# Gates and branch projections computed token-major, and a depthwise convolution issued tap by tap, in a three-layer hybrid block

## The chip, the cores and the metric

One core of a Trainium2 chip runs the whole program as one launch. The metric is the device time of one execution in microseconds (us); lower is better. TensorE (PE) does the matrix products, VectorE (DVE), ScalarE (ACT) and GpSimd (POOL) the rest; SP issues nearly all DMAs.

## The reference, cut to what matters

A sequence of 256 tokens of width 1024 goes through two layers of one kind (attention, gated linear attention and memory attention, then an MLP) and one layer of another (called layer 2 here: a spatial gate, a convolution and an attention). All three layers end their mixing part in the same way: three branches of width 512 are projected to 1024 columns, each is multiplied by a gate, the three are summed, and the sum is projected once more. In the first two layers the gate has a bias:

```python
gates = sigmoid(merge.reshape(B, S, 3, D) + b_merge)      # merge: 3072 of the columns of h @ w_in
merged = (gates[:, :, 0] * (o_nsa @ w_branch[0]) + gates[:, :, 1] * (o_gla @ w_branch[1])
          + gates[:, :, 2] * (o_mem @ w_branch[2]))
x = x + merged @ w_out
```

In layer 2 the gate is `sigmoid(h @ w_in[...])` without a bias, and branch 1 comes from a causal depthwise convolution over tokens, 31 taps on 512 channels, with a layer norm over the channels behind it.

## The kernel before, in words

**Precision and units.** Every product is done in three matmuls: both operands are split into a high part and a rest, `hi` and `lo`, and high times high, high times rest and rest times high are summed in PSUM (`mm3`, line 194). A weight arrives in a *unit*: 128 partitions of 1024 floats, 512 KB, one DMA from SP into `raw` (4 buffers). `split` (line 429) makes `hi` from it, on ACT or for every sixth unit on POOL (line 433), and `lo` by a subtraction on DVE (line 439), into 4 buffers each. While the convolution is being issued (`conv_on`), `hi` is never made on POOL, and every fourth subtraction goes to POOL (line 437).

**Two ways to multiply.** `tok_major` (line 489) holds 128 tokens of the activation in the array and streams weight columns past, up to 512 at a time, into two PSUM tiles (`acc`, 4 buffers), one for each half of the 256 tokens. `transposed` (line 503) holds 128 weight columns in the array and streams the 256 tokens past. A unit is consumed by 12 matmuls of 512 columns in the first way and by 24 of 256 in the second. The result of the second way has channels on the partitions, as the next product needs it; the result of the first has tokens there.

**Gates and branches.** `gates_of` (line 1123, layers 0 and 1) computes a gate of 1024 columns in four calls of `transposed`, 8 units in all; DVE scales the result by each token's norm (`RB`), and ACT takes the tanh with the bias (`CBH`, columns of `COL`, loaded as rows at the start). Layer 2 does the same at line 1587 without scale and bias. `merge_branch` (line 1135) projects a branch of 512 in four calls of `transposed`, 4 units in all. For each call DVE multiplies by the gate (line 1145 or 1147) and POOL adds into `M` (line 1148); on the last branch ACT and DVE split `M` into `mg`, which the output projection `out_proj` (line 1153, token-major) holds in the array, k after k. There are three gates and three branches in each of three layers.

**Order of the work.** PE's instructions run in the order written. The attentions and other side chains are generators; a planner (`clock`, `pump`, `start`, `finish`, `need`) counts an assumed time for each matmul and puts the next piece of a chain into PE's order when its assumed latency is over. The other engines' orders are made by a list scheduler at build time from priorities in program order, assumed durations and readiness, and are fixed from then on.

**The convolution.** `conv` (line 1427) is such a chain in layer 2. Its 120 taps run on DVE, all 30 of one channel block before those of the next, two for each step of the planner (1500 ns). Behind them stand the layer norm and the activation; the result is wanted before the last branch of layer 2 (`finish(c_conv)`, line 1592).

Of the kernel before, what the change touches and what calls it, by code (L numbers as in the profile page):

```python
# [10 lines left out]
F32 = mybir.dt.float32  # L11
# [87 lines left out]
def block_kernel(ctx, tc, x_in, mem_in, positions, ln_mix, w_in, b_merge, nsa_q_norm, nsa_k_norm,  # L99
# [173 lines left out]
    def load_rows():  # L273
# [3 lines left out]
        rows(48, 48, b_merge.rearrange("l b (k p) -> (l b k) p", p=P))  # L277
# [53 lines left out]
    CBH = consts.tile([P, 48], F32, name="CBH")  # L331
# [4 lines left out]
    def late_cols():  # L336
        pt = PS()
        tr(pt[:, :128], ROWB, IDF)
        dve.tensor_copy(COL[:, 48:128], pt[:, 48:128])
        dve.memset(COL[0:16, 102:110], 1.0)  # L340
        dve.memset(COL[64:80, 102:110], 1.0)
        dve.tensor_scalar(CBH, COL[:, 48:96], 0.5, None, op0=OP.mult)
# [84 lines left out]
    conv_on = [False]  # L427

    def split(hi, lo, raw):
        u = ucount[0]  # L430
        ucount[0] += 1
        if u % 6 == 5 and not conv_on[0]:
            pool.tensor_scalar(hi, raw, 1.0, 1.0, op0=OP.mult, op1=OP.mult)  # L433
        else:
            act(hi, raw, AF.Copy)  # L435
        if conv_on[0] and u % 4 == 0:
            pool.tensor_tensor(lo, raw, f32(hi), op=OP.subtract)  # L437
        else:
            dve.tensor_tensor(lo, raw, f32(hi), op=OP.subtract)  # L439
# [23 lines left out]
    def units(w2d, r0, nk, cols, paired=None, fine=False):  # L463
        n = sum(c1 - c0 for c0, c1 in cols)
        if paired:
            c0, c1 = cols[0]
            srcs = [(slice(64 * j, 64 * j + 64), 0, n,
                     w2d[256 * j:256 * j + 256, c0:c1].rearrange("(a d) n -> d a n", d=64)) for j in range(2)]
            h, lo = unit(srcs, 4, n)
            return [(h[:, j, :], lo[:, j, :]) for j in range(4)]  # L470
        per = max(1, 1024 // n)
# [17 lines left out]
    def tok_major(hh, hl, w2d, r0, nk, cols, fine=False):  # L489
        n = sum(c1 - c0 for c0, c1 in cols)  # L490
        ps = [ACC(), ACC()]
        ws = units(w2d, r0, nk, cols, None, fine)
# [630 lines left out]
    def gates_of(l, b, hh, hl, RB):  # L1123
        g = B8("gate")
        for c in range(4):
            ps = transposed(hh, hl, w_in[l], 0, 8, 3368 + 1024 * b + 256 * c, ACC())
            tmp = T2("gtmp", (2, 256))
            dve.tensor_tensor(tmp, v2(ps), RB[:, None, :].to_broadcast([P, 2, 256]), op=OP.mult)
            for j in range(2):
                cb = 2 * c + j  # L1130
                bc = l * 24 + b * 8 + cb
                act(g[:, cb, :], tmp[:, j, :], AF.Tanh, scale=0.5, bias=CBH[:, bc:bc + 1])
        return g

    def merge_branch(w2d, oT, g, M, last, mg, rows=None):
        oh, ol = oT
        first = M is None
        if first:
            M = B8("M")
        for c in range(4):  # L1140
            ps = transposed(oh, ol, w2d, 0, 4, 256 * c, ACC(), rows)
            cs = slice(2 * c, 2 * c + 2)
            fl = lambda t: t[:, cs, :].rearrange("p a b -> p (a b)")
            if first:
                dve.scalar_tensor_tensor(fl(M), fl(g), 1.0, ps, op0=OP.add, op1=OP.mult)
            else:
                dve.scalar_tensor_tensor(fl(g), fl(g), 1.0, ps, op0=OP.add, op1=OP.mult)  # L1147
                pool.tensor_tensor(fl(M), fl(M), fl(g), op=OP.add)  # L1148
                if last:
                    hilo(fl(mg[0]), fl(mg[1]), fl(M), 0.5)  # L1150
# [37 lines left out]
    def layer(l, hT):  # L1188
# [85 lines left out]
        for b in (2, 1, 0):  # L1274
            g = gates_of(l, b, hh, hl, RB)
# [101 lines left out]
    def layer_2(hT):  # L1377
# [49 lines left out]
        def conv():  # L1427
            conv_on[0] = True
            for cb in range(4):
                dve.tensor_scalar(CV[:, cb], GLU[:, cb, 0:256], CWT[:, cb, 0:1], COL[:, 110 + cb:111 + cb],  # L1430
                                  op0=OP.mult, op1=OP.add)
                for t in range(1, 31):
                    dve.scalar_tensor_tensor(CV[:, cb], GLU[:, cb, t:t + 256], CWT[:, cb, t:t + 1], CV[:, cb],
                                             op0=OP.mult, op1=OP.add)
                    if t % 2 == 0:
                        yield 1500.0
            conv_on[0] = False
            yield 1500.0
# [147 lines left out]
        for bi, b in enumerate((2, 0, 1)):  # L1586
            g = B8("gate")
            for c in range(4):
                ps = transposed(hh, hl, w, 0, 8, 5120 + 1024 * b + 256 * c, ACC())
                act(g[:, 2 * c:2 * c + 2, :], v2(ps), AF.Tanh, scale=0.5)  # L1590
# [92 lines left out]
```

## Time and profile before

| what | value |
|---|---|
| time, median of 3 runs (lowest to highest) | 1246.87 us (1245.86 to 1249.62) |
| the profiled execution's own time | 1243.95 us |
| its span, first to last instruction | 1242.2 us |
| PE busy, share of the span | 98% |
| weight loads of PE, DVE, ACT, POOL busy | 88%, 68%, 48%, 19% |
| matmuls | 8317 |
| mean granted TensorE clock | 0.995 of full |
| moved by DMA | 211 MB, 170 GB/s |

The busy time of PE counts modelled ends of pipelined matmuls, so two matmuls in a row overlap in it. What a matmul costs in a stream is the distance from its start to the next one's.

### The profile page before, as it was taken

To read this page: it belongs to the slowest core of one execution; us is meant where nothing else is said; L and a number is where in the kernel's file an instruction comes from. 1 tells how busy PE (TensorE), PEld (TensorE's weight loads), DVE (VectorE), ACT (ScalarE), POOL (GpSimd) and SP (SyncE) were. 2 spreads that over 40 slices of the span, in tenths; PEclk is the share of its full clock that TensorE was granted. 3 is DMA by queue.
4 is the path that set the end of the run, shared out by engine and by line. 5 is a ranking of instruction groups with operands and counts; after the bars stand their busy time and mean duration, and the time that the engine had idled before them with its cause. 6 is when DMAs were issued, how large, how long until landed. Compare 5 with 4: busy or idle time off the path is not lost. (4 is left out here: it accounts for less than half of the span.)

```text
span 1242.2 us, 21154 instructions
## 1 busy us (share of the span) xinstructions
PE 1216.0 (98%) x8317; PEld 1096.3 (88%) x8317; DVE 847.6 (68%) x1368; ACT 597.7 (48%) x957; POOL 239.8 (19%) x245
## 2 busy tenths in 40 slices
PE   8999999999999999999999999999999998999997
PEld 5897789998899898888689998989998987899996
DVE  5867888666745555667878557654545899955856
ACT  7567544444644344556654434534434334443542
POOL 2300220212112112200220023212211122110213
PEclk9999999999999999999999999999999999999999
DMA  8557523566566666656624565566665654455672
GB/s 277 173 159 204 157 91 109 171 183 214 167 187 184 193 185 189 184 157 171 188 69 115 154 187 185 173 200 180 193 190 170 199 154 131 134 173 169 186 218 72
DMA packets 165559, 211.00 MB, mean 170 GB/s; under 512 B 12065, under 2 KB 132277, under 8 KB 165460
## 3 DMA queue, kind: packets, MB, share of 16 engines
q1 hardware_dynamic: 165172, 209.49, 56.5%
q8 instruction: 65, 1.06, 0.4%
q0 software_dynamic: 288, 0.16, 0.1%
q14 instruction: 34, 0.28, 0.1%
HBM read 208.74 MB, written 1.05 MB: 169 GB/s over the span
## 5 line engine op out<-in xcount | busy, mean ns | idle before, releaser
L439 DVE TENSOR_TENSOR lo<-raw,hi 128x1024 fp32r<-128x1024 f32 (+1 forms) x359 | 451.0, 1262 | 263.8 <-ACT hi L435 211.9
L435 ACT ACTIVATE hi<-raw 128x1024 fp32r<-128x1024 f32 (+1 forms) x315 | 331.2, 1057 | 409.3 <-PE acc L188 248.7
L188 PE MATMUL acc<-hh,hi 128*128 128x256 f32 x960 | 278.1, 290 | 0.4 <-ACT hi L435 0.4
L188 PE MATMUL acc<-hh,lo 128*128 128x256 f32 x960 | 271.7, 283 | 1.5 <-DVE lo L439 1.0
L188 PE MATMUL acc<-hl,hi 128*128 128x256 f32 x960 | 271.6, 283 | 0.0
L188 PEld LDWEIGHTS acc<-hh,hi 128*128 128x128 f32 x960 | 183.8, 191 | 3.8 <-issue 2.3
L188 PEld LDWEIGHTS acc<-hh,lo 128*128 128x128 f32 x960 | 183.7, 191 | 1.9 <-DVE lo L439 1.2
L188 PEld LDWEIGHTS acc<-hl,hi 128*128 128x128 f32 x960 | 183.9, 192 | 1.0 <-DVE hl L528 0.2
L433 POOL TENSOR_SCALAR hi<-raw 128x1024 fp32r<-128x1024 f32 x54 | 65.6, 1215 | 476.4 <-PE acc L188 342.2
L188 PE MATMUL psm<-hh,hi 128*128 128x256 f32 x448 | 126.8, 283 | 0.0
L188 PE MATMUL psm<-hh,lo 128*128 128x256 f32 x448 | 126.8, 283 | 0.0
L188 PE MATMUL psm<-hl,hi 128*128 128x256 f32 x448 | 126.8, 283 | 0.0
L188 PE MATMUL acc<-hi,b8x 128*128 128x512 f32 (+1 forms) x336 | 103.9, 384 | 0.1
L188 PE MATMUL acc<-hi,oh 128*128 128x512 f32 x256 | 100.2, 391 | 0.0
L188 PE MATMUL acc<-lo,oh 128*128 128x512 f32 x256 | 99.8, 390 | 0.0
L188 PE MATMUL acc<-hi,ol 128*128 128x512 f32 x256 | 99.6, 389 | 0.0
L188 PE MATMUL acc<-hi,hh 128*128 128x512 f32 (+1 forms) x224 | 91.3, 408 | 0.0
L188 PE MATMUL acc<-lo,hh 128*128 128x512 f32 (+1 forms) x224 | 85.8, 383 | 2.2 <-DVE lo L439 2.2
L188 PEld LDWEIGHTS psm<-hh,hi 128*128 128x128 f32 x448 | 86.0, 192 | 0.5
L188 PEld LDWEIGHTS psm<-hl,hi 128*128 128x128 f32 x448 | 86.0, 192 | 0.5
L188 PEld LDWEIGHTS psm<-hh,lo 128*128 128x128 f32 x448 | 86.0, 192 | 0.0
L188 PE MATMUL acc<-hi,hl 128*128 128x512 f32 (+1 forms) x224 | 85.8, 383 | 0.0
(366 smaller groups left out, 2116.3 us busy)
## 6 DMA issues: line engine op xcount, KB each, us to landing
raw<-in_w_in SPq DMA_DIRECT2D x160, 512.0 KB
raw<-in_w_up SPq DMA_DIRECT2D x64, 512.0 KB
raw<-in_w_down SPq DMA_DIRECT2D x64, 512.0 KB
raw<-in_w_branch SPq DMA_DIRECT2D x28, 512.0 KB
raw<-in_w_out SPq DMA_DIRECT2D x24, 512.0 KB
raw<-in_cmp_w SPq DMA_DIRECT2D x32, 256.0 KB
raw<-in_mem_w_kv SPq DMA_DIRECT2D x15, 512.0 KB
raw<-in_w_branch SPq DMA_DIRECT2D x16, 256.0 KB
```

Source lines behind the costliest of these rows:

```text
L188: nc.tensor.matmul(o, l, r, start=start, stop=stop, skip_group_check=True)
L433: pool.tensor_scalar(hi, raw, 1.0, 1.0, op0=OP.mult, op1=OP.mult)
L435: act(hi, raw, AF.Copy)
L439: dve.tensor_tensor(lo, raw, f32(hi), op=OP.subtract)
```

## The change

`gates_of` and layer 2's gates become two calls of `tok_major` of 512 columns; the bias is brought into the gate's tile by a DMA on POOL's queue that repeats one row of 1024 floats on all partitions twice over, 1 MB of writes, and DVE adds it in the instruction that scales. The bias's old way (the 48 rows of `b_merge`, their columns in `COL`, and `CBH`) is taken out. `merge_branch` becomes two calls of `tok_major`; on the last branch DVE, not POOL, adds into `M`, and a new chain `merged_transposed` turns `M` back with 16 PE transposes before ACT and DVE split it. `paired` units (first two layers, last branch) are loaded 512 columns wide. `conv` issues one tap of all four channel blocks for each step of 5000 ns, and `split` no longer knows whether the convolution is on.

```diff
...
@@ -424,19 +421,15 @@
             pool.tensor_tensor(RC[:, ab, d0:d0 + 8], trig[:, 2, :], GB[:, 1, g0:g0 + 8], op=OP.mult)
 
     ucount = [0]
-    conv_on = [False]
 
     def split(hi, lo, raw):
         u = ucount[0]
         ucount[0] += 1
-        if u % 6 == 5 and not conv_on[0]:
+        if u % 6 == 5:
             pool.tensor_scalar(hi, raw, 1.0, 1.0, op0=OP.mult, op1=OP.mult)
         else:
             act(hi, raw, AF.Copy)
-        if conv_on[0] and u % 4 == 0:
-            pool.tensor_tensor(lo, raw, f32(hi), op=OP.subtract)
-        else:
-            dve.tensor_tensor(lo, raw, f32(hi), op=OP.subtract)
+        dve.tensor_tensor(lo, raw, f32(hi), op=OP.subtract)
 
     def unit(srcs, a, n, fine=False):
         raw = wraw.tile([P, 1024], F32, tag="raw", name=nm("raw"))
@@ -462,13 +455,17 @@
 
     def units(w2d, r0, nk, cols, paired=None, fine=False):
         n = sum(c1 - c0 for c0, c1 in cols)
+        per = max(1, 1024 // n)
         if paired:
             c0, c1 = cols[0]
-            srcs = [(slice(64 * j, 64 * j + 64), 0, n,
-                     w2d[256 * j:256 * j + 256, c0:c1].rearrange("(a d) n -> d a n", d=64)) for j in range(2)]
-            h, lo = unit(srcs, 4, n)
-            return [(h[:, j, :], lo[:, j, :]) for j in range(4)]
-        per = max(1, 1024 // n)
+            res = []
+            for k in range(0, 4, per):
+                srcs = [(slice(64 * j, 64 * j + 64), 0, n,
+                         w2d[256 * j + 64 * k:256 * j + 64 * (k + per), c0:c1].rearrange("(a d) n -> d a n", d=64))
+                        for j in range(2)]
+                h, lo = unit(srcs, per, n)
+                res += [(h[:, j, :], lo[:, j, :]) for j in range(per)]
+            return res
         res = []
         k = 0
         while k < nk:
@@ -486,10 +483,10 @@
             k += a
         return res
 
-    def tok_major(hh, hl, w2d, r0, nk, cols, fine=False):
+    def tok_major(hh, hl, w2d, r0, nk, cols, fine=False, paired=None):
         n = sum(c1 - c0 for c0, c1 in cols)
         ps = [ACC(), ACC()]
-        ws = units(w2d, r0, nk, cols, None, fine)
+        ws = units(w2d, r0, nk, cols, paired, fine)
         for k, (wh, wl) in enumerate(ws):
             need(hh, k)
             if fine and k == 0:
@@ -1120,34 +1117,51 @@
         dve.tensor_copy(rb, pt[:, 0:256])
         return rb
 
-    def gates_of(l, b, hh, hl, RB):
-        g = B8("gate")
-        for c in range(4):
-            ps = transposed(hh, hl, w_in[l], 0, 8, 3368 + 1024 * b + 256 * c, ACC())
-            tmp = T2("gtmp", (2, 256))
-            dve.tensor_tensor(tmp, v2(ps), RB[:, None, :].to_broadcast([P, 2, 256]), op=OP.mult)
-            for j in range(2):
-                cb = 2 * c + j
-                bc = l * 24 + b * 8 + cb
-                act(g[:, cb, :], tmp[:, j, :], AF.Tanh, scale=0.5, bias=CBH[:, bc:bc + 1])
+    def gates_of(l, b, hh, hl, rsd):
+        g = B8("gate", shape=(2, 1024))
+        nc.gpsimd.dma_start(g, wrap(b_merge[l, b], [[0, P], [0, 2], [1, 1024]]))
+        for h in range(2):
+            hs = slice(512 * h, 512 * h + 512)
+            c0 = 3368 + 1024 * b + 512 * h
+            ps = tok_major(hh, hl, w_in[l], 0, 8, [(c0, c0 + 512)])
+            for tt in range(2):
+                gs = g[:, tt, hs]
+                dve.scalar_tensor_tensor(gs, ps[tt], rsd[:, tt:tt + 1], gs, op0=OP.mult, op1=OP.add)
+                act(gs, gs, AF.Tanh, scale=0.5)
         return g
+
+    def merged_transposed(M, h, mg, prog):
+        yield 1500.0
+        for tt in range(2):
+            pt = PS()
+            for j in range(4):
+                tr(pt[:, j * P:j * P + P], M[:, tt, 512 * h + j * P:512 * h + j * P + P], IDF)
+            ks, ts_ = slice(4 * h, 4 * h + 4), slice(tt * P, tt * P + P)
+            hilo(mg[0][:, ks, ts_], mg[1][:, ks, ts_], v4(pt), 0.5)
+            if tt == 0:
+                yield 800.0
+        prog[0] = 4 * h + 4
 
     def merge_branch(w2d, oT, g, M, last, mg, rows=None):
         oh, ol = oT
         first = M is None
         if first:
-            M = B8("M")
-        for c in range(4):
-            ps = transposed(oh, ol, w2d, 0, 4, 256 * c, ACC(), rows)
-            cs = slice(2 * c, 2 * c + 2)
-            fl = lambda t: t[:, cs, :].rearrange("p a b -> p (a b)")
-            if first:
-                dve.scalar_tensor_tensor(fl(M), fl(g), 1.0, ps, op0=OP.add, op1=OP.mult)
-            else:
-                dve.scalar_tensor_tensor(fl(g), fl(g), 1.0, ps, op0=OP.add, op1=OP.mult)
-                pool.tensor_tensor(fl(M), fl(M), fl(g), op=OP.add)
-                if last:
-                    hilo(fl(mg[0]), fl(mg[1]), fl(M), 0.5)
+            M = B8("M", shape=(2, 1024))
+        prog = [0]
+        if last:
+            ready[id(mg[0])] = (mg[0], prog)
+        for h in range(2):
+            hs = slice(512 * h, 512 * h + 512)
+            ps = tok_major(oh, ol, w2d, 0, 4, [(512 * h, 512 * h + 512)], False, rows)
+            for tt in range(2):
+                gs, ms = g[:, tt, hs], M[:, tt, hs]
+                if first:
+                    dve.scalar_tensor_tensor(ms, gs, 1.0, ps[tt], op0=OP.add, op1=OP.mult)
+                else:
+                    dve.scalar_tensor_tensor(gs, gs, 1.0, ps[tt], op0=OP.add, op1=OP.mult)
+                    (dve if last else pool).tensor_tensor(ms, ms, gs, op=OP.add)
+            if last:
+                start(merged_transposed(M, h, mg, prog))
         return M
 
     def out_proj(w2d, mg, fin, gcol, mid=None):
@@ -1272,7 +1286,7 @@
         M = None
         mg = None
         for b in (2, 1, 0):
-            g = gates_of(l, b, hh, hl, RB)
+            g = gates_of(l, b, hh, hl, rsd)
             if b == 2:
                 oT = o_mem
                 finish(c_mem)
@@ -1425,17 +1439,14 @@
         CV, th8 = CVT[:, 0:4], CVT[:, 4:8]
 
         def conv():
-            conv_on[0] = True
             for cb in range(4):
                 dve.tensor_scalar(CV[:, cb], GLU[:, cb, 0:256], CWT[:, cb, 0:1], COL[:, 110 + cb:111 + cb],
                                   op0=OP.mult, op1=OP.add)
-                for t in range(1, 31):
+            for t in range(1, 31):
+                for cb in range(4):
                     dve.scalar_tensor_tensor(CV[:, cb], GLU[:, cb, t:t + 256], CWT[:, cb, t:t + 1], CV[:, cb],
                                              op0=OP.mult, op1=OP.add)
-                    if t % 2 == 0:
-                        yield 1500.0
-            conv_on[0] = False
-            yield 1500.0
+                yield 5000.0
             pm = PS()
             for cb in range(4):
                 mm(pm[:, 0:256], ONE, CV[:, cb], cb == 0, cb == 3)
@@ -1584,10 +1595,12 @@
         M = None
         mg = None
         for bi, b in enumerate((2, 0, 1)):
-            g = B8("gate")
-            for c in range(4):
-                ps = transposed(hh, hl, w, 0, 8, 5120 + 1024 * b + 256 * c, ACC())
-                act(g[:, 2 * c:2 * c + 2, :], v2(ps), AF.Tanh, scale=0.5)
+            g = B8("gate", shape=(2, 1024))
+            for h in range(2):
+                c0 = 5120 + 1024 * b + 512 * h
+                ps = tok_major(hh, hl, w, 0, 8, [(c0, c0 + 512)])
+                for tt in range(2):
+                    act(g[:, tt, 512 * h:512 * h + 512], ps[tt], AF.Tanh, scale=0.5)
             if bi == 2:
                 finish(c_conv)
                 dve.tensor_tensor(CV, CV, SB, op=OP.mult)
```

## Rows read from the trace of the kernel before

**Rows 1.** The page's head and its slices of the span

```profile
span 1242.2 us, 21154 instructions
PE 1216.0 (98%) x8317; PEld 1096.3 (88%) x8317; DVE 847.6 (68%) x1368; ACT 597.7 (48%) x957; POOL 239.8 (19%) x245
DVE  5867888666745555667878557654545899955856
```

**Rows 2.** The page's costliest groups: one matmul form of either width

```profile
L188 PE MATMUL acc<-hh,hi 128*128 128x256 f32 x960 | 278.1, 290 | 0.4 <-ACT hi L435 0.4
L188 PE MATMUL acc<-hi,oh 128*128 128x512 f32 x256 | 100.2, 391 | 0.0
```

**Rows 3.** Timeline of PE, a gate of layer 2: start, length, what, count

```profile
1176.54 0.28 PE L188 MATMUL acc<-hh,hi 128*128 128x256 f32 x1
...
1199.46 0.28 PE L188 MATMUL acc<-hh,lo 128*128 128x256 f32 x1
```

**Rows 4.** Timeline of PE, token-major projection of layer 1 with transposes in between

```profile
512.49 0.39 PE L188 MATMUL acc<-hi,hh 128*128 128x512 f32 x1
...
514.98 0.39 PE L188 MATMUL acc<-hi,hl 128*128 128x512 f32 x1
515.21 0.60 PE L192 MATMUL psm<-CF,X 128*128 128x128 f32 x4
515.56 0.49 PE L188 MATMUL acc<-hi,hh 128*128 128x512 f32 x1
515.89 0.39 PE L188 MATMUL acc<-lo,hh 128*128 128x512 f32 x1
```

**Rows 5.** Who PE waited for over the span: us in total, times, longest

```profile
PE acc L188 <- DVE lo L439: 4.0, 3, 2.2
PE psm L188 <- ACT pexp L1505: 3.1, 1, 3.1
```

**Rows 6.** Timeline of PE in the convolution stretch: the waits, in brackets

```profile
1018.69 0.50 PE L188 MATMUL acc<-lo,hh 128*128 128x512 f32 x1 [2.24 <-DVE lo L439]
...
1035.47 1.04 PE L188 MATMUL psm<-g,g 64*128 64x128 f32 x6 [3.14 <-ACT pexp L1505]
...
1080.20 0.39 PE L188 MATMUL acc<-hh,hi 128*128 128x256 f32 x1 [0.39 <-ACT hi L435]
...
1081.66 0.39 PE L188 MATMUL acc<-hh,lo 128*128 128x256 f32 x1 [0.95 <-DVE lo L439]
...
1083.91 0.39 PE L188 MATMUL acc<-hh,lo 128*128 128x256 f32 x1 [0.56 <-POOL lo L437]
```

**Rows 7.** Windows of the taps (line 1433): length, busy (count), PE clock, DMA share, GB/s

```profile
979.00:1019.00 40.00, 28.82 (x57) 1.00 0.52 153
1019.00:1060.00 41.00, 20.14 (x38) 0.92 0.50 152
```

**Rows 8.** Timeline of DVE: taps beside a POOL subtract, and alone

```profile
1012.11 5.38 DVE L1433 SCALAR_TENSOR_TENSOR b8x<-b8x,cw,b8x 128x256 f32<-128x256 f32 x8
...
1066.07 4.04 DVE L1433 SCALAR_TENSOR_TENSOR b8x<-b8x,cw,b8x 128x256 f32<-128x256 f32 x10
```

**Rows 9.** Groups of POOL: the weight subtracts during the convolution, and the branch sum

```profile
L1148 POOL TENSOR_TENSOR M<-M,gate 128x512 f32<-128x512 f32 x24 | 43.3, 1803 | 82.8 <-DVE gate L1147 77.2 <-ACT hi L435 5.5
L437 POOL TENSOR_TENSOR lo<-raw,hi 128x1024 fp32r<-128x1024 f32 x10 | 29.0, 2903 | 105.8 <-ACT hi L435 105.8
```

**Rows 10.** Windows: length, busy of PE, PEld, DVE, ACT, POOL (counts), clock, DMA

```profile
979.00:1010.00 31.00, 31.00 (x260) 31.00 (x260) 30.06 (x55) 12.46 (x14) 10.08 (x3) 1.00 0.55 163
1176.00:1199.00 23.00, 23.00 (x194) 23.00 (x194) 10.24 (x9) 7.82 (x9) 4.01 (x3) 1.00 0.58 173
```

**Rows 11.** Timeline of DVE at the end of layer 2's last branch

```profile
1205.78 0.68 DVE L528 SCALAR_TENSOR_TENSOR b8x<-M,b8x 128x512 fp32r<-128x512 f32 x1
1206.38 0.68 DVE L1147 SCALAR_TENSOR_TENSOR gate<-gate,acc 128x512 f32<-128x512 f32 x1
1206.98 1.21 DVE L439 TENSOR_TENSOR lo<-raw,hi 128x1024 fp32r<-128x1024 f32 x1
1210.04 0.69 DVE L528 SCALAR_TENSOR_TENSOR b8x<-M,b8x 128x512 fp32r<-128x512 f32 x1 [1.84 <-ACT b8x L527]
```

**Rows 12.** The page's DMA issues: KB each, median us to landing

```profile
DM<-const_d POOLq DMA_DIRECT2D x1, 96.0 KB, 4.2
```

More of the change, by code (lines that the diff above doesn't have):

```diff
@@ L275, in rows @@
             nc.sync.dma_start(ROWB[r0:r0 + n, :], src)
-        rows(48, 48, b_merge.rearrange("l b (k p) -> (l b k) p", p=P))
         rows(96, 2, gla_norm)
@@ L330, in block_kernel @@
     dve.tensor_copy(COL[:, 32:48], pt[:, 32:48])
-    CBH = consts.tile([P, 48], F32, name="CBH")
     GQK = consts.tile([P, 2], F32, name="GQK")
@@ L338, in late_cols @@
         tr(pt[:, :128], ROWB, IDF)
-        dve.tensor_copy(COL[:, 48:128], pt[:, 48:128])
+        dve.tensor_copy(COL[:, 96:128], pt[:, 96:128])
         dve.memset(COL[0:16, 102:110], 1.0)
         dve.memset(COL[64:80, 102:110], 1.0)
-        dve.tensor_scalar(CBH, COL[:, 48:96], 0.5, None, op0=OP.mult)
         dve.tensor_tensor(GQK, COL[:, 98:100], COL[:, 100:102], op=OP.mult)
```

## The prediction

> **What bounds the kernel now.** I read the head of the page first: PE is busy for 98% of the span, the next engine, DVE, for 68% [rows 1]. That alone is weak, since the page's matmul times overlap: the 256-column form is listed with a mean of 290 ns and the 512-column form with 391 [rows 2], which would make the narrow one look dear by half. The timeline gives the distances that count. In a gate of layer 2 the 192 matmuls from the first to the last of these rows start 22.92 us apart, 0.1200 us for each of the 191 steps [rows 3]. In a token-major projection twelve matmuls of 512 columns lie between 512.49 and the transposes at 515.21, 0.2267 us each [rows 4]. Neither stretch has a wait in it. The list of who PE waited for confirms it: the two largest entries of the whole span are 4.0 and 3.1 us [rows 5]. So this kernel is bound by PE's stream, nearly everywhere, and an edit is worth what it takes out of that stream. The exception is the convolution of layer 2, where DVE is busy for 30.06 of 31 us [rows 10] and PE waits for it.
>
> **Part 1, the width of the matmuls: a gain.** A unit of weights took 24 matmuls of 256 columns, 24 x 0.1200 = 2.880 us, and takes 12 of 512, 12 x 0.2267 = 2.720 us. The columns streamed are the same; two narrow matmuls cost 0.240 and the wide one in their place 0.227. The saving is 0.160 us a unit. Nine gates of 8 units and nine branches of 4 make 108 units: 108 x 0.160 = **17.3 us**. The upper bound is this; the lower one is no saving, if the wide form ran at 0.240.
>
> Here a page of the Trainium skill speaks against the change. In "TensorE: Matmul & The Clock Gate", section "Back-to-back issue gap", the distance of two matmuls at full clock is the columns divided by 2.4 GHz plus some 2.5 ns. By that, an estimate from the page, a unit would save 24 x 109.2 - 12 x 215.8 = 31 ns, and the 108 units 3.3 us. The rows show 120.0 and 226.7 ns instead, about 13 ns over the columns' time in both widths, and I go by them.
>
> **Part 2, turning M back: a cost on PE.** The channel-major form came out of the old order for nothing; now 16 transposes a layer stand in PE's order, four groups of four, twelve groups in all. The rows have just such a group inside a stream of 512: four transposes from 515.21 to 515.56, 0.35 us, and the matmul behind them takes 0.33 until the next one instead of 0.227 [rows 4]. That is 0.45 us a group, 12 x 0.45 = **5.4 us**, and nothing hides it.
>
> **Part 3, waits where M is handed over: a cost.** The planner puts the transposes of the first token half about 2.7 us behind the last matmul of a projection half, those of the second about 1.4 us later, whether DVE is ready or not. DVE must do gate and add for either half: spaced as these instructions are, 0.6 us each (1205.78 to 1206.38) [rows 11], 1.2 us for the first half and 2.4 for both, after some 0.2 us until the last sum is out. Without anything ahead it makes both. A weight subtraction that the fixed order puts ahead costs 1.2 us [rows 11]; with two of them ahead, and the gates of both halves before the adds, the first half is ready at 0.2 + 2 x 1.2 + 3 x 0.6 = 4.4 us, 1.7 too late. So a group waits between 0 and 1.7 us. Behind the last group, ACT and DVE (0.6 us each) must be done before the output projection's fifth k, which comes 8 triples of 0.68 us plus the two groups, 6.3 us, behind the projection: a wait of 0 to 2 us a layer. I take 1 us a layer, **3 us**, near the lower end since PE has most often not waited at such places before; both ends go into the range. The add that moves from POOL (1.8 us on average [rows 9]) to DVE (0.6) shortens this chain; in a branch of 10.9 us of PE, DVE has 4 x (0.6 + 0.6 + 0.6) + 4 x 1.2 = 12.0 us against 10.9 + 1.8 of PE with the transposes: full, but not over.
>
> **Part 4, the convolution: a gain.** PE's waits in its stretch are 2.24 + 3.14 + 0.39 + 0.95 + 0.56 = 7.3 us [rows 6]. Behind the first two, the granted clock falls: its mean is 0.92 in 41 us [rows 7], a loss of 0.08 x 41 = 3.3 us of PE's time at half of full clock (1.2 GHz in place of 2.4). Together 10.6 us. What stands behind the waits is in the DVE rows: ten taps alone take 4.04 us, eight beside a subtraction on POOL 5.38, where 3.2 would do [rows 8]: 2.1 us late, in an order fixed without it, and the weight rest that PE needed came after. POOL did ten such subtractions, of 2.9 us [rows 9]. The change takes all ten away and gives DVE ten of 1.2 [rows 11], 12 us, spread over the stage; POOL gets back its sixth `hi`, 1.2 us, on an engine with time. The taps themselves stay 120; the new step only lowers their priority, and a scheduler that goes by readiness may issue them as early as before (57 were done in the first 40 us [rows 7], where two for each 1500 ns would make 53). So DVE stays nearly full to about the old end. I take 8 of the 10.6 us, three of four, since one POOL subtraction lies ahead of each of the waits; the bounds are 0 and 10.6.
>
> **What costs nothing.** The bias comes as six DMAs of 1 MB on POOL's queue. The nearest row is POOL's 96 KB, landed in 4.2 us [rows 12]; with 1 MB at the kernel's mean of 170 GB/s, 6 us, that is about 10. For two gates of a layer the tile is free only when POOL has done the last add, some 4 us after the branch; the bias lands at about 14, the first gate half needs it at 4 x 2.72 = 10.9. DVE may stand there for 3 us with subtractions queued behind it; the four prepared units (10.9 us of PE) cover that. Without this cover it would be 4 x 3 = 12 us. Behind the DMA on POOL stands at most a `hi` whose unit is two or more ahead. ACT's tanh, half as many and twice as wide, and the small edits at the start lie beside PE; DVE in a gate is busy for 10.24 of 23 us [rows 10].
>
> **The sum.** -17.3 + 5.4 + 3 - 8 = -16.9 us. Made against the profiled execution's own 1243.95 us it gives 1227; the median of the three runs lies 2.9 us above that execution, and on it the forecast is 1246.87 - 16.9 = **1230.0 us**.
>
> **Rivals.** (a) *The taps don't spread.* DVE stays full as in [rows 10], other instructions come late in its fixed order, and part 4 is worth nothing: 1246.87 - 8.9 = 1238.0. For it: taps need nothing but the tap before, so readiness holds none back. Against it: each wait in [rows 6] has a POOL subtraction ahead. (b) *Slower: the handover of M.* Its place is the twelve groups of part 3. If DVE comes with two subtractions ahead at each, 12 x 1.7 + 3 x 2 = 26.4 us in place of 3: -17.3 + 5.4 + 26.4 - 8 = +6.5, 1253.4. It decides from about 20 us of such waits on. For it: PE's order is fixed and waits where it stands. Against it: DVE has held such a chain before, with POOL's slower add in it, and still idles 1.84 us inside it [rows 11]. (c) *The width saves nothing*: a wide matmul of a gate takes 0.240. Then 0 + 5.4 + 3 - 8 = +0.4, 1247.3; [rows 4] speak against it, being the same form on the same operands. By the Trainium skill's spacing named in part 1 it would be 1244.
>
> **Chances and range.** The forecast 0.67, (a) 0.17, (b) 0.08, (c) 0.03, something else 0.05. A measurement of this kernel tells about 0.3% from no change, 3.7 us. The forecast and (a) are both faster by more, 0.84; (b) is slower, 0.08; (c) and the rest count as the same, 0.08. For the range: with parts 3 and 4 at their best ends the gain is 17.3 - 5.4 + 10.6 = 22.5, 1224.4; at the other side it takes in (a) with 3 us more of handover, 1241. Below, a little is added for chains that also close up: 1223 to 1241.
>
> **What would show it.** Right: matmuls of 512 columns 0.227 apart in the gates, about 1300 of them in place of 2600 narrow ones; twelve groups of transposes of M, 0.45 us each; no clock below full between 1000 and 1050 us; no line of POOL subtracting weights. Part 3 wrong: waits of PE for the split of `mg`, or of the transposes for DVE's add, over 1 us a layer. Part 4 wrong: taps beside waits of PE for `lo` still. The whole would be wrong if PE came to wait for the bias, seen as DVE standing before the gate's instruction for a DMA, or for the convolution's end ahead of the last branch.

## The result, and the profile after

The kernel before took 1248.05 us (median of 4 runs, 1245.86 to 1249.62), the changed one **1230.49 us** (4 runs, 1227.59 to 1235.59): ratio 0.9865, 95% interval [0.9827, 0.9902], 17.6 us faster. The forecast was 1230.0 us in 1223 to 1241. The profiled execution of the changed kernel took 1227.59 us, its span is 1225.8 us; it is the fastest of the four, and that matters below.

The page's head, to be read against [rows 1]; below it the slices of the granted clock:

```profile
span 1225.8 us, 18640 instructions
PE 1200.9 (98%) x7069; PEld 1028.4 (84%) x7069; DVE 852.6 (70%) x1389; ACT 583.1 (48%) x926; POOL 213.7 (17%) x236
...
PEclk9999999999999999999999999999999999999998
```

PE is still busy for 98%, with 1248 fewer matmuls: the kernel is bound by the same stream, which has become shorter. The timeline of PE in layer 2 (start, length, what) shows 41 matmuls of 512 columns without a wait, 9.07 us from the first start to the last, 0.2267 us a step:

```profile
1118.79 0.39 PE L188 MATMUL acc<-lo,oh 128*128 128x512 f32 x1
...
1127.86 0.39 PE L188 MATMUL acc<-hi,hl 128*128 128x512 f32 x1
```

A group of transposes of M in layer 0's last branch, same view, to be read against [rows 4]. From the transposes to the second matmul behind them it is 0.67 us; without them it would be 0.227, so a group costs 0.44:

```profile
278.89 0.60 PE L192 MATMUL psm<-CF,M 128*128 128x128 f32 x4
279.25 0.48 PE L188 MATMUL acc<-hi,oh 128*128 128x512 f32 x1
279.56 0.39 PE L188 MATMUL acc<-lo,oh 128*128 128x512 f32 x1
```

The windows of the convolution stretch (length, busy and count of PE, PEld, DVE, ACT, POOL, granted clock, DMA share, GB/s), to be read against [rows 7, 10]; first two of the kernel before, then the changed one:

```profile
979.00:1019.00 40.00, 37.76 (x289) 36.18 (x289) 39.06 (x68) 16.21 (x18) 12.88 (x4) 1.00 0.52 153
1019.00:1060.00 41.00, 37.86 (x227) 31.69 (x226) 40.17 (x86) 15.88 (x38) 7.10 (x6) 0.92 0.50 152
```

```profile
979.00:1010.00 31.00, 31.00 (x244) 30.28 (x243) 30.05 (x56) 11.49 (x13) 4.10 (x2) 1.00 0.57 171
...
979.00:1019.00 40.00, 40.00 (x287) 37.27 (x286) 39.05 (x73) 15.76 (x18) 4.10 (x2) 1.00 0.59 176
1019.00:1060.00 41.00, 39.84 (x299) 35.47 (x298) 39.56 (x85) 17.51 (x41) 7.83 (x6) 1.00 0.47 142
```

DVE is as full as before (30.05 of 31 us; it was 30.06). What changed is PE: busy for 40.00 of 40 us (it was 37.76), and the clock stays at 1.00 in the second window, where its mean was 0.92. So the time came out of the waits for DVE, not out of DVE's load.

Who PE waited for, over the span (us in total, times, longest), to be read against [rows 5]:

```profile
PE psm L192 <- DVE kss L579: 2.9, 1, 2.9
PE psm L188 <- DVE a L1054: 2.5, 5, 1.3
PE acc L188 <- ACT hi L444: 2.1, 1, 2.1
...
PE psm L188 <- ACT pexp L1516: 1.2, 1, 1.2
...
PE acc L188 <- ACT b8x L524: 0.8, 1, 0.8
...
PE acc L188 <- DVE b8x L525: 0.6, 1, 0.6
...
PE acc L188 <- DVE lo L432: 0.4, 2, 0.2
```

The two entries that led this list before are down from 4.0 to 0.4 (`lo`) and from 3.1 to 1.2 (`pexp`). New at the top is `kss`, a wait before the very first projection, which was 1.4 before; the entries for `b8x` are the handover of M in layer 2.

DVE waited for a bias load twice, before the first half of the third gate in each of layers 0 and 1 (timeline of DVE, in brackets the wait):

```profile
260.08 1.41 DVE L1129 SCALAR_TENSOR_TENSOR gate<-acc,xrs,gate 128x512 f32<-128x512 f32 x2 [2.27 <-DMA gate<-in_b_merge]
...
732.61 1.41 DVE L1129 SCALAR_TENSOR_TENSOR gate<-acc,xrs,gate 128x512 f32<-128x512 f32 x2 [2.92 <-DMA gate<-in_b_merge]
```

PE waited for nothing in these stretches (190 to 282 and 665 to 755 us).

For all that follows the span is cut where certain matmuls of PE start: the first of layer 0's projection of X, the first of each layer's first branch, the first of each output projection, the first projection of the next layer. The stretches between, in us, from the profiled execution of each kernel ("to b" ends at the first branch, "b to o" is three branches and two gates, "o on" the output projection and the MLP):

| kernel | start | L0 to b | L0 b to o | L0 o on | L1 to b | L1 b to o | L1 o on | L2 to b | L2 b to o | L2 o on | span |
|---|---|---|---|---|---|---|---|---|---|---|---|
| before | 36.8 | 159.9 | 85.67 | 230.2 | 159.5 | 85.66 | 206.3 | 163.1 | 84.1 | 31.1 | 1242.2 |
| after | 39.1 | 159.3 | 82.35 | 230.0 | 159.5 | 82.35 | 206.8 | 151.7 | 81.6 | 33.1 | 1225.8 |
| after minus before | +2.3 | -0.6 | -3.3 | -0.2 | 0.0 | -3.3 | +0.5 | -11.4 | -2.5 | +2.0 | -16.4 |

Where nothing in a stretch was edited, it repeats to 0.1 us from kernel to kernel, with three exceptions. The start is one, of which more below. The second are the attention stretches of layers 0 and 1: in some executions the clock falls to half there for 3.41 or 6.83 us (in ten of the other eleven profiled executions, not in these two), and a stretch with such a spell is 0.9 to 3.5 us longer; that scatter is left out of the readings below. The third are layer 2's branches, which take 84.07 us in the kernel before and in no_pool_sub and 85.4 in conv_only and tap_order, for a reason that stays open; in the kernels with the new gates they and the last stretch hang on one late weight, as the last experiments show.

The two stretches "o on" of layers 0 and 1 now hold two groups of transposes each, 0.85 us (turn_twice, below), and yet are 0.2 shorter and 0.5 longer. So some 1.4 us of small waits that the kernel before has in these two output projections are gone; no run isolates what took them away.

### The profile page after: what moved, and what is told of

It reads as the page before. It is cut to its first block, busy times and chain, and to the rows that moved or that the text cites. A ratio compares the mean times of both kernels' runs of the same rounds, so it can differ in the third digit from the quotient of the medians.

```text
span 1225.8 us, 18640 instructions
## 1 busy us (share of the span) xinstructions
PE 1200.9 (98%) x7069; PEld 1028.4 (84%) x7069; DVE 852.6 (70%) x1389; ACT 583.1 (48%) x926; POOL 213.7 (17%) x236
## 5 line engine op out<-in xcount | busy, mean ns | idle before, releaser
L188 PE MATMUL acc<-hi,hh 128*128 128x512 f32 (+1 forms) x512 | 205.7, 402 | 0.0
L188 PE MATMUL acc<-hi,hl 128*128 128x512 f32 (+1 forms) x512 | 197.1, 385 | 0.0
L188 PE MATMUL acc<-lo,hh 128*128 128x512 f32 (+1 forms) x512 | 196.7, 384 | 0.0
L188 PEld LDWEIGHTS acc<-hi,hh 128*128 128x128 f32 x512 | 96.4, 188 | 20.4 <-issue 4.0
L188 PEld LDWEIGHTS acc<-hi,hl 128*128 128x128 f32 x512 | 96.1, 188 | 19.4
L188 PE MATMUL acc<-hh,hi 128*128 128x256 f32 x384 | 111.8, 291 | 0.0
L188 PEld LDWEIGHTS acc<-lo,hh 128*128 128x128 f32 x512 | 96.5, 188 | 16.3
L188 PE MATMUL acc<-hh,lo 128*128 128x256 f32 x384 | 108.7, 283 | 0.2 <-DVE lo L432 0.2
L188 PE MATMUL acc<-hl,hi 128*128 128x256 f32 x384 | 108.8, 283 | 0.0
L188 PEld LDWEIGHTS acc<-hi,oh 128*128 128x128 f32 x400 | 75.2, 188 | 14.8
```

The costliest lines, as they stand in the source:

```text
L188: nc.tensor.matmul(o, l, r, start=start, stop=stop, skip_group_check=True)
```

## Experiments

### The two parts apart

gates_only is the changed kernel with the convolution and the weight split of before; conv_only is the kernel before with the new convolution and split.

```diff
 # conv_only, in split() of the kernel before
-        if u % 6 == 5 and not conv_on[0]:
+        if u % 6 == 5:
...
-        if conv_on[0] and u % 4 == 0:
-            pool.tensor_tensor(lo, raw, f32(hi), op=OP.subtract)
-        else:
-            dve.tensor_tensor(lo, raw, f32(hi), op=OP.subtract)
+        dve.tensor_tensor(lo, raw, f32(hi), op=OP.subtract)
 # and in conv()
-                for t in range(1, 31):
+            for t in range(1, 31):
+                for cb in range(4):
...
-                    if t % 2 == 0:
-                        yield 1500.0
+                yield 5000.0
```

> The changed kernel with the convolution and the weight split of before (taps block by block, every fourth subtraction on POOL while it runs). My theory: the gates and branches alone are worth 17.3 us of PE less 5.4 for the transposes and the waits of the handover, about 6 us net of the span before (1242.2), so a span of about 1236; the stretch from layer 2's first product to its first branch is long again, 151.7 us in the changed kernel, about 162 here, with waits of PE behind POOL's subtractions. Rival: the gates and branches carry the whole gain; span about 1226 and the stretch near 152.

> The kernel before with the new convolution and the new weight split alone. My theory: the stretch of layer 2 up to its first branch falls from 163.1 us to about 153, and nothing else moves: span about 1232. Rival (a) of the prediction, that the taps don't spread and DVE's order stays as bad: span 1240 or more.

Measured: gates_only 1236.87 us, ratio 0.9915 [0.9897, 0.9932]; conv_only 1239.61 us, 0.9934 [0.9917, 0.9952]; before, in these rounds, 1247.42. Taken alone the parts bring 10.6 and 7.8 us, together 18.4; the whole change brought 17.6. Within the scatter of the runs they add. In layer 2's stretch to the first branch the convolution edits take 163.05 to 152.93 in conv_only, and between gates_only and the changed kernel 161.82 to 151.70: **10.1 us in both settings**. (The profiled execution of conv_only has a half-clock spell in each of the two attentions, which are 2.4 and 2.3 us longer, its start is 1.5 us later, and layer 2's branches take 1.3 more; so its span, 1239.7, missed the 1232 that was expected, though the stretch did not.)

### Which of the two convolution edits

no_pool_sub is the kernel before with the split of the change alone, tap_order with the new order and pacing of the taps alone; the two diffs above, one each.

> The kernel before with one of the two convolution edits: every remainder of the split stays on VectorE while the taps run, the order and pacing of the taps stay those of before. If the subtracts on GpSimd beside the taps cost the time (theory), the stretch from the first projection of layer 2 to its first branch goes from 163.1 us to about 153 and the span from 1242 to about 1232, with no tap above 1.3 us. If it is the order of the taps (rival), the stretch stays at about 163 and the span at 1242, long taps or not. If VectorE's extra remainders (24 more of 0.49 us or so) push the taps back, the stretch lies between.

> The kernel before with the other of the two convolution edits: the taps go tap by tap over the four channel blocks with the new pacing, the remainders of every fourth unit stay on GpSimd while they run. If the subtracts cost the time (theory), the stretch from the first projection of layer 2 to its first branch stays within 2 us of 163.1 and the span near 1242, with taps of 2 us and more still there. If the order of the taps does it (rival), the stretch goes to about 153 and the span to about 1232.

Measured: no_pool_sub 1237.54 us, ratio 0.9917 [0.9902, 0.9932]; tap_order 1248.26 us, 1.0009 [0.9998, 1.0020]. The stretch is 152.93 us in the first, 162.73 in the second. The order of the taps is worth nothing here; all 10.1 us come with the new split. That edit does two things: it takes the subtractions off POOL, and it gives POOL back every sixth `hi`. No run parts them; but before, PE waited for a `hi` of ACT for only 0.39 us in this stretch [rows 6]. PE's waits fall from 7.3 us [rows 6] to 1.4, and the clock, whose mean was 0.92 in a window of 41 us, is not below full: 5.9 + 3.3 = 9.2 of the 10.1 us. The waits of PE between 960 and 1100 us, first of no_pool_sub, then of tap_order:

```profile
PE psm L188 <- ACT pexp L1499: 1.2, 1, 1.2
PE acc L188 <- DVE lo L435: 0.2, 1, 0.2
```

```profile
PE psm L188 <- ACT pexp L1504: 4.9, 1, 4.9
PE acc L188 <- DVE lo L439: 2.3, 1, 2.3
PE acc L188 <- POOL lo L437: 1.0, 1, 1.0
```

The groups of DVE in the same stretch (count, busy us, mean ns, idle before), the kernel before and no_pool_sub:

```profile
L1433 DVE SCALAR_TENSOR_TENSOR b8x<-b8x,cw,b8x 128x256 f32<-128x256 f32 x120 | 65.4, 594 | 0.2
L439 DVE TENSOR_TENSOR lo<-raw,hi 128x1024 fp32r<-128x1024 f32 x33 | 40.1, 1219 | 10.3 <-ACT hi L435 9.3 <-POOL hi L433 0.9
```

```profile
L1428 DVE SCALAR_TENSOR_TENSOR b8x<-b8x,cw,b8x 128x256 f32<-128x256 f32 x120 | 54.0, 493 | 0.5
L435 DVE TENSOR_TENSOR lo<-raw,hi 128x1024 fp32r<-128x1024 f32 x44 | 53.5, 1217 | 8.4 <-ACT hi L434 6.5 <-POOL hi L432 1.9
```

Taps and weight rests together are 105.5 us before and 107.5 without POOL: DVE did not get less to do (eleven more rests of 1.22 us, where the expectation had written 24 of 0.49). The subtractions that POOL took over cost DVE nearly what they saved it (11.4 us of longer taps against 13.4 us of work), and they came late: 2.9 us each on POOL [rows 9], and behind them the next rest on DVE, 2 us late [rows 8]. It is the lateness that PE paid for: the wait of 2.24 us at 1018.69 ends with the rest that stood behind the eight taps of [rows 8].

How a tap gets long shows in two rows of tap_order, POOL's timeline and then DVE's (start, length):

```profile
1052.92 2.40 POOL L437 TENSOR_TENSOR lo<-raw,hi 128x1024 fp32r<-128x1024 f32 x1 [18.72 <-ACT hi L435]
```

```profile
1053.00 2.60 DVE L1434 SCALAR_TENSOR_TENSOR b8x<-b8x,cw,b8x 128x256 f32<-128x256 f32 x1
```

The tap starts 0.08 us after the subtraction and ends 0.28 us after the subtraction's end, at 1055.60 against 1055.32: its end hangs on the subtraction's, so it stood rather than ran slowly. In the kernel before the same is seen at seven of the eight subtractions between 980 and 1095 us: one tap of 2.03 to 2.64 us at each, which ends 0.28 us behind it. The Trainium skill, "SBUF — State Buffer", section "Who interferes with whom", says that a VectorE instruction with two inputs in SBUF contends with a GpSimd instruction that reads SBUF; this trace agrees, with 2.60 us for a tap that takes 0.49 on average when POOL makes no subtraction.

### The width of the matmuls

narrow is the changed kernel, token-major as it is, with every matmul of the gates and branches cut into two of 256 columns.

```diff
-                mm3(ps[tt][:, :n], hh[:, k, ts_], hl[:, k, ts_], wh, wl, k == 0, k == nk - 1)
+                if halved:
+                    for q in range(2):
+                        qs = slice(256 * q, 256 * q + 256)
+                        mm3(ps[tt][:, qs], hh[:, k, ts_], hl[:, k, ts_], wh[:, qs], wl[:, qs], ...)
...
```

> The changed kernel with gates and branches still token-major, but each matmul of 512 columns cut into two of 256 (the same unit then takes 24 matmuls). If the gain is the width of the matmuls, 108 units cost 0.160 us more each: 17.3 us above the changed kernel's span of 1225.8, about 1243, and matmuls 0.120 us apart. If it is the layout, or the work of the other engines that the layout saves, the span stays near 1226.

Measured: 1242.85 us, ratio 0.9962 [0.9950, 0.9975]; against the 1247.42 of the kernel before in these rounds, 4.6 of the 17.6 us are left. The stretches of two gates and three branches, 28 units, are 86.51 us in layers 0 and 1, 4.16 more than in the changed kernel: 0.149 us a unit against the predicted 0.160. Summed over all stretches but the first and the last, narrow is 14.3 us longer (1237.74 - 38.06 - 31.75 against 1225.82 - 39.08 - 33.11). Of this 1.1 lie in layer 1's attention, where the profiled execution of narrow has a half-clock spell of 3.41 us, so 13.2 are left. On the other side the changed kernel loses 1.0 us to a wait in layer 2's branches (81.62 us; 80.63 without it, in norm_early below) and 1.4 in the last stretch, which narrow passes in 31.75 us: PE, being slower, waits for nothing behind 1090 us. So the width, where nothing else waits, is worth about **14 us of the 17.3**. Where the rest is: the one gate that lies inside the attention of layers 0 and 1 should have given 8 x 0.160 = 1.28 us each, and gave 0.6 and 0.0. In layer 1, PE waited there for DVE and ACT for 0.7 + 0.6 + 0.2 = 1.5 us before and for 2.4 after; the waits between 620 and 685 us in the changed kernel are

```profile
PE psm L188 <- DVE a L1054: 1.3, 1, 1.3
PE psm L192 <- DVE ck L827: 0.8, 1, 0.8
PE psm L188 <- ACT pts L934: 0.3, 1, 0.3
```

In narrow they sum to 1.2. A faster gate beside an attention chain that sets the end only moves PE's time into its waits; for layer 0, whose waits are 2.3 us before and 2.4 after, the missing 0.7 us stays open.

### The transposes of M, and the handover

turn_twice does the transposes of M twice into the same tile; pool_add puts the last branch's add back on POOL.

```diff
 # turn_twice
+            for _ in range(2):
                 for j in range(4):
                     tr(pt[:, j * P:j * P + P], M[...], IDF)
 # pool_add
-                    (dve if last else pool).tensor_tensor(ms, ms, gs, op=OP.add)
+                    pool.tensor_tensor(ms, ms, gs, op=OP.add)
```

> The changed kernel with the 16 transposes of M in each layer done twice over into the same place. My theory: nothing hides them, four transposes are 0.35 us and the pipeline change behind them isn't paid again: 12 x 0.35 to 12 x 0.45, 4.2 to 5.4 us above 1225.8, about 1230.5. Rival: PE waits at the handover anyway (for DVE or for the split of M), and the second transposes lie in that wait: under 1.5 us more.

> The changed kernel with the last branch's add of M on GpSimd instead of VectorE, which lengthens the chain from the last matmul to the transposed sum. By the chain as the prediction summed it (theory), each of the 6 halves of M becomes about 1.2 us later and what is not covered by the next matmuls is paid: 2 to 6 us in all, most of it in the stretches behind the last branch (85.7 plus 230 us in layer 0, 85.7 plus 206 in layer 1, 31 in layer 2). If the handover is as fragile as the rival of the prediction has it, over 10 us. If it is all hidden, nothing.

Measured: turn_twice 1235.19 us, ratio 0.9903 [0.9885, 0.9921], 4.7 us above the changed kernel by the medians, in which start and attentions scatter; pool_add 1232.01 us, 0.9878 [0.9858, 0.9899]. By stretches, doubling costs 0.85 us in each of the four stretches of layers 0 and 1 that hold two groups (82.35 to 83.20, 82.35 to 83.19, 229.99 to 230.84, 206.79 to 207.64): 0.42 a group, as read off the timeline. In layer 2 it costs nothing (81.47 and 33.06 against 81.62 and 33.11): turn_twice lists no wait of PE behind 1185 us, so the second transposes fill what was a wait. So the transposes are **3.4 us** in layers 0 and 1, and layer 2's four groups come out of a wait as long as there is one. In norm_early (below) there is none, and layer 2's two stretches are together 2.8 us shorter than before (80.63 + 31.71 against 84.07 + 31.09), where its 28 units should save 4.3 (narrow's 84.93 less 80.63): there the four groups cost about 1.5. The slower add costs 1.5 us by the medians, which the scatter of either kernel's runs exceeds; by stretches, against the changed kernel, it is 0.3 (L0 b to o), 0.1 (L0 o on), 1.0 (L1 o on) and 1.0 (L2 o on), less 0.2 in layer 2's branches. That is at or below the low end of what was expected: the handover is nowhere near the 20 us at which it would have decided.

### The two loads that came at a bad time

norm_early loads the two vectors of the last norm (512 KB each) ahead of layer 2's gates, into tiles of their own, and no longer between the weights of the last output projection. bias_late holds back the first bias load until the masks are through POOL, by a one-column write into its tile. both_moves has both; after_again is the changed kernel once more.

```diff
 # norm_early
+        LGA, LGB = G4(1), G4(1)
+        nc.sync.dma_start(LGA[:, 0], wrap(ln_g_2[0], [[0, P], [1, 1024]]))
+        nc.sync.dma_start(LGB[:, 0], wrap(ln_b_2[0], [[0, P], [1, 1024]]))
...
-        LGT = B8("hh", shape=(2, 1024))
-        nc.sync.dma_start(LGT[:, 0], wrap(ln_g_2[0], [[0, P], [1, 1024]]))
-        nc.sync.dma_start(LGT[:, 1], wrap(ln_b_2[0], [[0, P], [1, 1024]]))
 # bias_late, in gates_of()
+        if l == 0 and b == 2:
+            pool.tensor_copy(g[:, 0, 0:1], f32(MLR[:, 1151:1152]))
         nc.gpsimd.dma_start(g, wrap(b_merge[l, b], [[0, P], [0, 2], [1, 1024]]))
```

> The changed kernel with the two last-norm vectors (2 times 512 KB) loaded ahead of layer 2's gates, into two tiles of their own, and no longer just ahead of the last output projection's weights. If those transfers made the w_out unit late on which ScalarE and behind it the split of M stood (theory), the last stage goes from 33.1 us to 31.2 or so, the unit lands in 4 to 5 us instead of 8.4, and the span falls by 2. If ScalarE stands for another reason (rival: the transposes of M come too late in any case), the last stage stays at 33.1. The two transfers in their new place cost nothing by either.

> The changed kernel with the first of the six bias loads (1 MB, issued at 19.6 us) held back until the masks are through GpSimd, some 45 us later; the other five as they are. Theory: that load is what makes the first normalisation late, so TensorE's wait for it before the first projection falls from 1.6 to 3.2 us (six kernels with the early load) to 1.3 to 1.4 (four without it), and the time falls by about 1.2 us, a little more where the long wait also brought the half clock. The load, landing near 73 us, is still 60 us and more ahead of its first use, so nothing is paid there. Rival: the start differs for another reason, and the wait stays above 2.

> The changed kernel itself, once more, beside the two versions of this call, to compare them on one chip: 1227.6 to 1235.6 us, median near 1230.5, and again 1.6 us or more of waiting before the first projection and about 2.9 us of waits for ScalarE in the last stage.

> The changed kernel with both loads moved: the first bias later, the two vectors of the last norm earlier. If both theories hold and the gains add, 1.2 us at the start and 1.4 to 2.4 at the end: a median near 1227, below the changed kernel by about 3 us. If one gain is only shifted to a later wait, 1 us or less.

Measured: norm_early 1229.28 us, ratio 0.9857 [0.9835, 0.9879]. In other rounds, side by side on one chip: bias_late 1227.26 us (1226.94 to 1227.43), 0.9827 [0.9804, 0.9851]; after_again 1230.86 us (1229.20 to 1234.48), 0.9852 [0.9828, 0.9876]; both_moves **1224.99 us** (1224.81 to 1227.09), 0.9813 [0.9789, 0.9838]. The last is the fastest version here, 22.4 us below the kernel before (1247.35 in these rounds) and 5.9 below the changed one.

*The end.* The chain of waits of the changed kernel, in order of time, between 1178 and 1200 us (start, length, what):

```profile
1181.58 0.46 SPq L1615
...
1182.09 0.43 SPq L1616
...
1182.62 8.39 DMA raw<-in_w_out
...
1191.12 1.07 ACT hi L431
...
1192.21 1.22 DVE lo L432
1193.43 0.61 DVE b8x L525
```

SP issues the two vectors, then a unit of `w_out` that lands 8.39 us after its issue. ACT runs in order, stands on the `hi` of that unit, and the split of `mg` (`b8x`, line 524) stands behind it; on DVE the `lo` of the same unit is ahead of `b8x`. PE pays 0.83 and 0.64 us:

```profile
1192.71 0.50 PE L188 MATMUL acc<-hi,b8x 128*128 128x512 f32 x1 [0.83 <-ACT b8x L524]
...
1194.09 0.73 PE L188 MATMUL acc<-hi,b8x 128*128 128x512 f32 x2 [0.64 <-DVE b8x L525]
```

In norm_early the same chain between 1184 and 1206 us is PE alone, ACT's longest wait for a unit of `w_out` there is 1.32 us instead of 3.11, and the last stretch takes 31.71 us. With 80.63 instead of 81.62 us in the branches ahead of it that is 2.4 us; the median fell by 1.2 against the first runs of the changed kernel, and by 2.3 between bias_late and both_moves, which ran side by side. The expectation of after_again is wrong in one thing: of the 2.9 us of waits for ScalarE that it places in the last stretch, 2.1 (`hi` L444) lie in the first 40 us. What is left at the handover is 0.6 + 0.6 us in after_again, and the last stretch took 33.14 us again. gates_only shows how near the edge this is: there SP issues three units of `w_out` ahead of the two vectors instead of two, PE waits for nothing behind 1185 us, and the two stretches take 80.63 and 31.72 us, as in norm_early.

*The start.* The same pattern. ACT's timeline, of after_again and then of bias_late (in brackets the wait ahead):

```profile
30.73 1.06 ACT L431 ACTIVATE hi<-raw 128x1024 fp32r<-128x1024 f32 x1 [4.58 <-DMA raw<-in_w_in]
31.70 1.18 ACT L524 ACTIVATE hh<-psm,COL 128x256 fp32r<-128x256 f32 x3
```

```profile
26.41 1.06 ACT L431 ACTIVATE hi<-raw 128x1024 fp32r<-128x1024 f32 x1 [0.77 <-DMA raw<-in_w_in]
27.38 0.46 ACT L524 ACTIVATE hh<-psm,COL 128x256 fp32r<-128x256 f32 x1
```

The 1 MB bias, issued at 19.78 us in after_again and landed at 27.93, is in flight together with the first weights of `w_in`, which SP issues from 23.26 us on; ACT stands on one of these for 4.58 us (0.77 where the bias comes later), and the split of X (`hh`), already in PSUM, stands behind it. The profile names `kss` on DVE as what PE waits for; that instruction is itself behind the split. PE's waits there:

```profile
PE psm L192 <- DVE kss L579: 4.4, 1, 4.4
```

```profile
PE psm L192 <- DVE kss L579: 1.3, 1, 1.3
```

Over all profiled executions this wait is 1.3 to 1.4 us in the six without the early bias load (before, conv_only, no_pool_sub, tap_order, bias_late, both_moves) and 1.6 to 4.4 in the seven with it. Behind 4.40 us of waiting the clock also fell: in after_again the window from 33 to 40 us is granted 0.51 of full speed. So the price is more than the wait, and it differs from run to run: the stretch "start" is 1.9 us shorter in bias_late (37.15) than in the first profiled execution of the changed kernel and 6.0 shorter than in after_again (43.12); by the medians of bias_late and after_again it is 3.6 us, with a spread of 0.5 us in bias_late against 5.3 in after_again. Both are more than was expected (1.2 us for bias_late, 3 for both_moves, which gained 5.9).

## Why the prediction was right

The time was right to half a microsecond, by a sum whose terms were not:

| term | predicted | shown | by |
|---|---|---|---|
| part 1, width | -17.3 | about -14 | narrow |
| part 2, transposes | +5.4 | +3.4 in layers 0 and 1, about +1.5 in layer 2 | turn_twice, norm_early |
| part 3, handover | +3 | +2.4 in layer 2, none seen in layers 0 and 1 | norm_early |
| part 4, convolution | -8 | -10.1 | gates_only, conv_only, no_pool_sub |
| the first bias load | 0 | +1.9 in the profiled execution, 3.6 by medians | bias_late |
| small waits in two output projections | 0 | about -1.4 | the stretches alone |
| sum | -16.9 | about -16, with the 1.9 | measured: -16.4 by spans, -17.6 by medians |

That parts 1 to 4 have the right signs, and most of them nearly the right size, is no luck. That the sum hit to half a microsecond is: 3 us too much for the width and 1.9 forgotten at the start stand against 2 too little for the convolution, 1.1 too much for parts 2 and 3 and 1.4 that was not reckoned with. The four runs of the changed kernel alone spread over 8 us (1227.59 to 1235.59).

*Part 1.* The mechanism and the spacing hold, with 0.2267 us for the wide form. The spacing in the Trainium skill, "TensorE: Matmul & The Clock Gate", section "Back-to-back issue gap", which the page gives for the gap of an isolated matmul and by which the width would have saved an estimated 3.3 us, does not agree with narrow, which shows about 14. The size was off because "108 x 0.160" multiplied over every stage, though the prediction itself read that PE's stream bounds the kernel only "nearly everywhere". A unit is worth 0.149 us in the stretches of layers 0 and 1 where nothing waits, and two of the nine gates lie inside an attention, where the change gained 0.6 and 0.0 us in place of 1.28 each.

*Part 2.* 0.44 us a group was right. "Nothing hides it" holds for layers 0 and 1; in layer 2 the groups lie in time that PE would otherwise wait for the split of M.

*Part 3.* Between 0 and 2 us a layer was right, 1 us in each was not: it is 2.4 in layer 2 (listed as waits of 0.83 and 0.64) and nothing in the others. It lies at the first k of the output projection, not at the fifth, and its cause was another. The text reckoned with DVE's subtractions ahead of the add; what stood ahead was ACT, on a late weight. Rival (b), the handover as the slower case, was priced by DVE with two subtractions ahead at each of twelve groups; pool_add, which lengthens just this chain, costs 1.5 us by the medians.

*Part 4.* The gain came near its upper bound, 10.6, by the mechanism that [rows 8] show (taps beside a POOL subtraction); no_pool_sub gets all of it without the new order. The step "DVE stays nearly full to about the old end" was right: the taps end at 1083 us, as they ended at 1085. Taking three quarters of the gain for that reason was the mistake, and rival (a) made it whole: its condition came true, the taps did not spread, and yet the gain was paid in full. A DVE that is busy for 30.05 of 31 us cost PE nothing there, since the rests came in time.

*What costs nothing.* DVE stood for a bias twice, 2.27 and 2.92 us, close to the 3 us that the text allowed, and as it said the prepared units covered that: PE has no wait there, and the stretch is 82.35 us also in gates_only, where DVE stood for 7.3 us in all. So the sign that the text had named for a wrong whole, DVE standing before the gate's instruction for a DMA, was seen, and PE did not come to wait by it. The loads landed 7.6 us after their issue (median), where 10 was reckoned. The first of the six loads was not costed as a transfer: the text asked only whether the bias itself lands in time, not which weights land later for it.

## What to carry to other kernels

Cost a new load by what it delays, not by when it is needed itself: an engine that runs in order stands on the late weight, and everything behind it stands too, ready or not. A subtraction moved to GpSimd to relieve VectorE relieved it of almost nothing here (13.4 us of work against 11.4 us of longer taps), since VectorE's own two-input instructions ran beside it; judge such a move by when each result comes, not by busy time. A saving per instruction is paid only where that engine's stream sets the end, so multiply it stage by stage.

## What the runs showed of the hardware that was not expected

Beside a GpSimd instruction on 128x1024 not every tap stands, but at most one. It ends 0.28 us after that instruction, whatever its length: 1.28 us beside a `hi` of 1.06 (started 0.06 us earlier, at 1008.84 in the changed kernel), 2.60 beside the subtraction of 2.40. Taps that end earlier take their usual 0.48 us, and then it is GpSimd that takes longer: the subtraction at 1000.13 in the kernel before, beside four such taps and a weight rest of 1.22, took 4.75 us and held the next tap for 2.63. So GpSimd is slow beside taps too: its `hi` takes 2.04 us on average in no_pool_sub's convolution stretch and 1.06 at 23 us in the changed kernel, where no tap runs.

Half-clock spells of 3.41 us or twice that came also without a long wait of TensorE ahead. The windows of both_moves (columns as above) show one at 632.65, in layer 1's attention, behind 2.60 us in which TensorE was busy throughout, with matmuls of 16 columns for the most part:

```profile
630.00:632.60 2.60, 2.60 (x24) 2.60 (x24) 0.06 (x1) 1.29 (x8) 0.00 (x0) 1.00 0.03 12
632.65:636.06 3.41, 3.41 (x14) 1.84 (x12) 2.76 (x12) 0.90 (x2) 0.00 (x0) 0.50 0.00 0
```

The changed kernel's first profiled execution has the same four waits of PE between 600 and 640 us (0.9, 0.8, 0.3 and 0.2) and no such spell. Why one execution has it there and another not stays open.
